# A decoder trunk on one core: projection weights laid out by the host, and one DVE addition per chain replaced by an adding transfer from DRAM

## The chip, the core and the metric

The kernel runs on one core of one Trainium2 chip. The time is device microseconds of one execution, and the kernel is timed several times; the median counts. The engines are called PE (TensorE, the matrix products), PEld (its weight loads, which overlap PE), DVE (VectorE), ACT (ScalarE), POOL (GpSimd) and SP (SyncE). Each works through its own instructions in order. A transfer is issued by SP, ACT or POOL and then done by the 16 DMA engines; "landing" is the moment at which a transfer's completion can be seen.

## The reference

Two layers over 512 tokens of 1024 features, all in float32. Layer 0 mixes tokens by attention, layer 1 by a gated linear recurrence; after each comes a gated feed-forward part with a causal convolution. Cut to what the change touches:

```python
def dilated_attention_mixer(x, w_qkv, w_o, rel_bias):
    qkv = (x @ w_qkv).reshape(B, S, N_GROUPS, 3, HEADS_PER_GROUP, HEAD_DIM)
    ...
def rglru_mixer(x, w_in, ...):
    h = x @ w_in
    ...
def conv_ffn(x, w_up, conv_w, conv_b, w_down):
    u = causal_dwconv(x @ w_up, conv_w, conv_b)      # w_up: 1024 x 6144
    g, v = u[..., :D_FF], u[..., D_FF:]
    return (jax.nn.gelu(g, approximate=True) * v) @ w_down

def reference(...):
    for layer in range(DEPTH):                       # DEPTH = 2
        h = rms_norm(x, norm_mix_pre[layer])
        h = dilated_attention_mixer(h, ...) if layer % 2 == 0 else rglru_mixer(h, ...)
        x = x + rms_norm(h, norm_mix_post[layer])
        h = conv_ffn(rms_norm(x, norm_ffn_pre[layer]), ...)
        x = x + rms_norm(h, norm_ffn_post[layer])
    return x
```

## The kernel before

**Three passes per product.** A weight block of 128 x 512 float32 numbers is split in two: ACT copies it to a rounded high part (`whi`, L169), DVE subtracts that from the block and so gets the low part (`wlo`, L170). Activations are split in the same way. Each product is three matmuls, high by high, high by low and low by high.

**Chunks and their plan.** The weights come in chunks of 1 MB, 8 KB in each of the 128 partitions, in a fixed order (`plan`). `load()` issues a chunk's transfer on SP into a tile `raw`, of which there are three; a chunk may be loaded once the chunk three before it has been split to the end. For a column chunk (`w_cols`) a tile holds 256 columns of the weights: 8 pieces of 256 numbers (1 KB) in a partition. For the attention's columns this takes two transfers per chunk. `pump()` takes the next piece of a chunk and emits its split; there are 14 half buffers for split parts.

**The chains.** In each feed-forward part, 9 of the 12 column groups, with both halves (gate and value), are computed by `seven()` in 18 chains. A chain takes one chunk, seen as four blocks, 128 columns by 512 rows each: `w11` and `w12` (first 128 columns, upper and lower rows), `s1` and `a22` (last 128 columns, upper and lower rows). Seven block products with sums of blocks stand in for eight. The sums on the weights' side are formed in place in `raw`, in the order of `stream()`:

- `ahead`: `s1` becomes s1+a22, by a transfer that reads the block a22 from DRAM and adds it to what lies in SBUF (POOL issues it, L206);
- `left`: once `w11` is split, `w11` becomes w11+s1 by another such transfer;
- the piece `s1` is split, and then `across` makes `s1` the sum of w11 (by now w11+s1) and a22, on DVE (L230);
- the piece `s2` is the split of that sum; after it `lower` adds it to `w12` on DVE (L234), for the piece `s4`.

**What sets the order.** The order is written out: `AT` and `CYCLE` give each of a chain's seven product steps a slot (12 matmuls each), `free_slots` fills the slots between with other work, and at each slot `tick()` emits the next splits. The chains 3 to 8 have nine used slots, the others ten. So DVE's, ACT's and POOL's orders are fixed when the program is built. The step that multiplies `a22` adds to a bank of PSUM after DVE has read that bank at L1100; PE's line is L1082, and ACT copies partial results out at L1091. L812, L816 and L834 are the convolution and the activation that follow a chain, L838 the product of gate and value.

Of the kernel before, what the change touches and what calls it, by code (L numbers as in the profile page):

```python
# [15 lines left out]
ALU = mybir.AluOpType  # L16
AX = mybir.AxisListType

P = 128
S = 512  # L20
D = 1024
KD = D // P
HEADS = 8
HD = 128
D_FF = 3 * D
# [13 lines left out]
SEVEN = range(3, 12)  # L39
# [14 lines left out]
def _bucket(dist):  # L54
    max_exact = BUCKETS // 2
    d = np.maximum(dist, 1).astype(np.float64)
    large = max_exact + (
        np.log(d / max_exact) / np.log(MAX_DISTANCE / max_exact) * (BUCKETS - max_exact)
    ).astype(np.int32)
    large = np.minimum(large, BUCKETS - 1)  # L60
    return np.where(dist < max_exact, dist, large).astype(np.int32)


def _runs(g):

    at, step, n, dist = ((128, 1, 129, 1), (256, 1, 128, 4), (256, 4, 32, 16))[g]
    b = _bucket(np.arange(n) * dist)
    runs, i = [], 0
    while i < n:
        k = i + 1  # L70
        while k < n and b[k] == b[i]:
            k += 1
        if k == i + 1:
            while k < n and b[k] == b[k - 1] + 1 and (k + 1 == n or b[k + 1] != b[k]):
                k += 1
            runs.append((at + i * step, step, k - i, int(b[i]), True))
        else:
            runs.append((at + i * step, step, k - i, int(b[i]), False))
        i = k
    return runs  # L80


@with_exitstack
def kernel(
# [25 lines left out]
    nc = tc.nc  # L110
# [61 lines left out]
    plan = []  # L172
    state = {"dma": 0, "cv": 0, "used": 0, "live": 0, "next": 0, "hold": False, "even": False, "quiet": False}
# [3 lines left out]
    def parts_of(kind, raw):  # L177

        if kind == "feat":
            return [raw[:, :, m * P : (m + 1) * P] for m in range(2)]  # L180
        if kind == "value":
            return [raw[:, 2 * i : 2 * i + 2, :] for i in range(raw.shape[1] // 2)]
        if kind == "rows":
            return [raw[:, i : i + 1, :] for i in range(2)]
        return [raw]
# [11 lines left out]
    def blocks(i):  # L197

        raw = raws[i]
        return {  # L200
            n: raw[:, 4 * k : 4 * k + 4, m * P : m * P + P]
            for n, m, k in (("w11", 0, 0), ("w12", 0, 1), ("s1", 1, 0), ("a22", 1, 1))
        }

    def add_rows(to, src):
        nc.gpsimd.dma_start(to, src, accum_op=ALU.add)  # L206

    def ahead(i):
        assert i < state["dma"]
        add_rows(blocks(i)["s1"], plan[i][3][0][0][:, 4:8, P:256])  # L210

    def free_slots(n):

        end = CYCLE * n
        free = [CYCLE * c + r for c in range(n) for r in ((6, 7, 9) if c < 3 or c > 8 else (6, 7))][2:] + [end, end + 1]
        assert not {CYCLE * c + a for c in range(n) for a in AT.values()} & set(free)
        return free

    def stream(i0, n):

        items = []
        for c in range(n):
            i, o = i0 + c, CYCLE * c

            def left(i=i):
                add_rows(blocks(i)["w11"], plan[i][3][0][0][:, 0:4, P:256])

            def across(i=i):
                x = blocks(i)
                nc.vector.tensor_tensor(x["s1"], x["w11"], x["a22"], op=ALU.add)  # L230

            def lower(i=i):
                x = blocks(i)
                nc.vector.tensor_tensor(x["w12"], x["w12"], x["s1"], op=ALU.add)  # L234

            if c:
                items.append((o - 7, (None, lambda i=i: ahead(i))))
            for at, item in (
                (-6, ("w11", "w11")), (-5.9, (None, left)), (0, ("s1", "s1")), (0.4, ("w12", "w12")),
                (1.5, (None, across)), (5, ("s2", "s1")), (5.1, (None, lower)), (7, ("s3", "w11")),  # L240
                (8.5, ("s4", "w12")), (10.6, ("a22", "a22")),
            ):
                if isinstance(item[0], str):
                    item = ((i, item[0]), lambda i=i, h=item[1]: [blocks(i)[h]], item[0] == "a22")
                items.append((o + at, item))
        free = free_slots(n)
        direct = up["direct"]
        at = 8
        for key, loads, cuts, length in direct:
            u = free[at]  # L250
            if loads:
                items.append((u - EARLY, (None, loads)))
            items.append((u - 1, ((i0, key), cuts, False)))
            at += length
        return [item for _, item in sorted(items, key=lambda x: x[0])]

    def strided_stream(i0):

        items = []
        for r in range(4):  # L260
# [27 lines left out]
            for u in range(4):  # L288
                i = i0 + 6 * r + 4 + u // 2

                def cuts(i=i, m=u % 2):
                    raw = parts_of("value", raws[i])[m]
                    return [raw[:, :1], raw[:, 1:]]

                items.append((ROUND * r + QUARTERS[u if r == 3 else 4 * u], ((i, u % 2), cuts, u % 2 == 1)))
# [124 lines left out]
        while sides:  # L420
            tick()

    def w_cols(w, c0, normed=False, kind="feat"):
        if normed:
            srcs = [(w[i * 512 : (i + 1) * 512, c0 : c0 + 256].rearrange("(p k) c -> p k c", k=4), 4) for i in range(2)]
        else:
            srcs = [(w[:, c0 : c0 + 256].rearrange("(k p) c -> p k c", p=P), KD)]
        plan.append((kind, KD, 256, srcs))

    def w_value(w, *cuts):  # L430

        for i in range(2):
            rows = w[i * 512 : (i + 1) * 512, :]
            plan.append(("value", 4, 512, [(rows[:, c0 : c0 + n].rearrange("(p k) c -> p k c", k=4), n) for c0, n in cuts]))

    def w_rows(w, c):
        r0 = 256 * c
        plan.append(("rows", 2, D, [(w[r0 : r0 + 256, :].rearrange("(k p) c -> p k c", p=P), 2)]) + (True,) * (c == 3))
# [717 lines left out]
    def attention(hT, post, pre):  # L1156
        rowv = [dp.tile([8, TOE], F32, name=f"rowv{g}") for g in range(3)]

        def biases():
            rb = bp.tile([8, 3, BUCKETS], F32, tag="rb", name="rb")  # L1160
            for g in range(3):
                nc.sync.dma_start(rb[:, g], rel_bias[:, 8 * g : 8 * g + 8].rearrange("b h -> h b"))
            yield 1
            for g in range(3):
                row = gen(s="row")[:8, :TOE]
                nc.gpsimd.memset(row, NEG)
                for at, step, n, b, each in _runs(g):
                    src = rb[:, g, b : b + n] if each else rb[:, g, b : b + 1].to_broadcast([8, n])
                    nc.gpsimd.tensor_copy(row[:, at : at + (n - 1) * step + 1 : step], src)
                nc.gpsimd.dma_start(rowv[g], row)  # L1170
                yield 4 if g == 2 else 1
            yield from feature_columns()
# [492 lines left out]
        gate_out(3)  # L1665
        return run()

    qkv, w_in = attn_w_qkv[0], lru_w_in[0]
    for hp in range(4):
        if hp % 2 == 0:  # L1670
            w_value(qkv, (2 * D + hp * 256, 512))
        for j in range(2):
            w_cols(qkv, j * D + hp * 256, True)
    for hp in range(4):
        for g, j in ((1, 0), (1, 1), (2, 0), (2, 1)):
            w_cols(qkv, g * 3 * D + j * D + hp * 256, True, "quad")
        w_value(qkv, *((g * 3 * D + 2 * D + hp * 256, 256) for g in (1, 2)))
    for c in range(4):
        w_rows(attn_w_o[0], c)
    for layer in range(2):  # L1680
        if layer:
            lru_parts = [("x", 0), ("x", 1), ("x", 2), ("g", 0), ("x", 3), ("g", 1), ("g", 2), ("g", 3)]
            for kind, n in lru_parts + [("b", n) for n in range(4)]:
                if kind == "g":
                    plan.append(("gate", 4, 256, [(w[0, n].rearrange("(k p) c -> p k c", p=P), 2) for w in (lru_ga_w, lru_gx_w)]))
                else:
                    w_cols(w_in, n * 256 + (D if kind == "b" else 0))
            for c in range(4):
                w_rows(lru_w_out[0], c)
        for j, half in [(j, half) for j in range(12) for half in range(2)]:  # L1690
            w_cols(ffn_w_up[layer], half * D_FF + j * 256, kind="seven" if j in SEVEN else "feat")
        for half, k in [(1, k) for k in range(0, TAIL, 4)] + [(0, REST[0])] + [(1, k) for k in range(TAIL, 24, 4)]:
            rows = ffn_w_down[layer][k * P : (k + 4) * P, half * 512 : half * 512 + 512]
            plan.append(("value", 4, 512, [(rows.rearrange("(k p) c -> p k c", p=P), 512)]))
# [85 lines left out]
```

## Time and profile before

| | |
|---|---|
| median of 3 runs | 1399.64 us (1399.26 to 1400.11) |
| the profiled execution | 1398.78 us, of which the span is 1397.0 us |
| PE busy | 1383.6 us, 99% of the span |
| PEld, DVE, ACT, POOL busy | 92%, 80%, 57%, 16% |
| granted TensorE clock | 0.999 |
| moved by DMA | 202.05 MB, mean 145 GB/s |

How to read it: the span runs from the first instruction to the last; a busy share is an average over stages, so the stage around the change is read by itself. The attention stage lasts to about 490 us, the first feed-forward part to about 865 us, with its 18 chains on PE from 542 to 782 us; the recurrence to about 1000 us, the second feed-forward part to the end, with chains from 1074 to 1314 us. A row of the timeline gives the start, the time from there to the end, the engine, the line and the instruction, `xN` for N in a row, and in brackets the idle time before it and what ended it. A row of the waits gives the total, the number of times and the longest.

### The profile page before, as it was taken

Reading aid. Unit: us, or ns where it says so; the run is one execution under the profiler, and the core shown is the slowest. Engines: PE = TensorE matmul, PEld = TensorE weight load, DVE = VectorE, ACT = ScalarE, POOL = GpSimd, SP = SyncE. Lnnn points to the kernel's source line nnn. Section 1 sums busy time; section 2 is a strip of 40 time slices with the busy share of each in tenths; the row PEclk is TensorE's granted clock in tenths of the full one; section 3 lists DMA queues with packets and bytes.
Section 4 is the critical chain, followed back from the end, with each engine's and each line's share of the span. In section 5 each row is a group of like instructions: output and inputs, shape, how many; then the busy total and the mean of one; then the engine's idle time right before and its main releaser. Section 6 shows DMA issues by size and latency. Waiting matters only on the chain.

```text
span 1397.0 us, 25641 instructions
## 1 busy us (share of the span) xinstructions
PE 1383.6 (99%) x9797; PEld 1285.1 (92%) x9797; DVE 1121.6 (80%) x2201; ACT 789.7 (57%) x1646; POOL 225.6 (16%) x344
## 2 busy tenths in 40 slices
PE   9999999999999999999999999999999999999998
PEld 7989998999998899999999888989899999999886
DVE  6576898888866889999888759769889999888853
ACT  7343565454536556656666545489556666666641
POOL 0341341222210102212110001000101222111000
PEclk9999999999999999999999999999999999999999
DMA  7644464747574645767663542431444776665511
GB/s 231 180 141 122 122 183 107 222 125 204 147 220 139 204 159 106 165 151 163 133 147 96 185 147 76 136 122 61 151 151 99 161 157 159 160 135 126 175 55 61
DMA packets 171892, 202.05 MB, mean 145 GB/s; under 512 B 10561, under 2 KB 141081, under 8 KB 171513
## 3 DMA queue, kind: packets, MB, share of 16 engines
q1 hardware_dynamic: 123064, 153.34, 34.4%
q0 software_dynamic: 47856, 46.02, 18.1%
q8 instruction: 77, 1.26, 0.4%
q10 hardware_dynamic: 848, 1.05, 0.2%
q14 instruction: 47, 0.38, 0.1%
HBM read 181.41 MB, written 18.96 MB: 143 GB/s over the span
## 4 chain that ended last, share of the span: by engine, by line
PE 82%; DVE 9%; ACT 5%; issue 2%; DMA 1%; POOL 0%; DVEq 0%; ACTq 0%; POOLq 0%
PE ps L1082 29%; PE acc L444 24%; PE ps L444 15%; PE v L1279 7%; DVE wlo L170 4%; ACT whi L169 1%; PE v L1217 1%; DVE u L816 1%; DVE xb L1583 1%; PE O L1491 1%; PE S L1425 1%; PE S L1373 1%; ACT sig L1604 1%; PE tr L537 1%; PE O L444 0%
## 5 line engine op out<-in xcount | busy, mean ns | idle before, releaser
L170 DVE TENSOR_TENSOR wlo<-raw,whi 128x512 fp32r<-128x512 f32 x616 | 406.4, 685 | 109.2 <-ACT whi L169 106.6
L169 ACT ACTIVATE whi<-raw 128x512 fp32r<-128x512 f32 x616 | 365.3, 626 | 156.7 <-PE acc L444 51.2
L444 PE MATMUL ps<-hT,whi 128*128 128x256 f32 x1632 | 281.6, 277 | 1.3 <-ACT whi L169 1.3
L444 PEld LDWEIGHTS ps<-hT,whi 128*128 128x128 f32 x1632 | 247.1, 188 | 2.2 <-ACT whi L169 1.5
L444 PE MATMUL ps<-hT,wlo 128*128 128x256 f32 x816 | 225.4, 276 | 0.4 <-DVE wlo L170 0.4
L1082 PE MATMUL ps<-T,whi 128*128 128x256 f32 x1248 | 221.8, 277 | 0.0
L1082 PE MATMUL ps<-hT,whi 128*128 128x256 f32 x1248 | 220.7, 276 | 0.0
L1082 PEld LDWEIGHTS ps<-T,whi 128*128 128x128 f32 x1248 | 191.5, 188 | 3.0
L1082 PEld LDWEIGHTS ps<-hT,whi 128*128 128x128 f32 x1248 | 190.0, 188 | 2.0
L1082 PE MATMUL ps<-T,wlo 128*128 128x256 f32 x624 | 172.5, 276 | 0.0
L1082 PE MATMUL ps<-hT,wlo 128*128 128x256 f32 x624 | 172.1, 276 | 0.0
L206 POOL DMA_DIRECT2D raw<-in_ffn_w_up_dram x72 | 92.8, 1319 | 409.0 <-DVE wlo L170 278.3
L444 PEld LDWEIGHTS ps<-hT,wlo 128*128 128x128 f32 x816 | 153.4, 188 | 0.6 <-DVE wlo L170 0.6
L444 PE MATMUL acc<-whi,ahi 128*128 128x512 f32 x336 | 131.4, 391 | 0.0
L444 PE MATMUL acc<-whi,alo 128*128 128x512 f32 x336 | 131.0, 390 | 0.2
L444 PE MATMUL acc<-wlo,ahi 128*128 128x512 f32 x336 | 130.8, 389 | 0.0
L1082 PEld LDWEIGHTS ps<-T,wlo 128*128 128x128 f32 x624 | 117.2, 188 | 0.0
L1082 PEld LDWEIGHTS ps<-hT,wlo 128*128 128x128 f32 x624 | 117.2, 188 | 0.0
L1279 PE MATMUL v<-whi,hT 128*128 128x512 f32 x320 | 107.0, 397 | 0.0
L1091 ACT ACTIVATE part<-ps 128x256 f32<-128x256 f32 x156 | 59.0, 378 | 79.8 <-PE ps L1082 76.9
L816 DVE SCALAR_TENSOR_TENSOR u<-ps,cols,u 128x511 f32<-128x511 f32 x120 | 89.4, 746 | 4.5 <-ACT u L812 2.4
L812 ACT ACTIVATE u<-ps,cols 128x512 f32<-128x512 f32 x60 | 46.3, 776 | 61.9 <-DVE ps L1095 50.9
(224 smaller groups left out, 2511.4 us busy)
## 6 DMA issues: line engine op xcount, KB each, us to landing
raw<-in_ffn_w_up_dram SPq DMA_DIRECT2D x48, 1024.0 KB
raw<-in_attn_w_qkv_dram SPq DMA_DIRECT2D x67, 512.0 KB
raw<-in_ffn_w_up_dram POOLq DMA_DIRECT2D x72, 256.0 KB, 4.9
raw<-in_ffn_w_down_dram SPq DMA_DIRECT2D x14, 1024.0 KB
dw<-in_ffn_w_down_dram SPq DMA_DIRECT2D x40, 256.0 KB
raw<-in_lru_w_in_dram SPq DMA_DIRECT2D x8, 1024.0 KB
turned<-T POOLq DMA_DIRECT2D x26, 256.0 KB, 2.6
ft<-turned POOLq DMA_DIRECT2D x104, 64.0 KB, 5.1
```

What stands on the lines that cost most here:

```text
L169: nc.scalar.activation(hi, raw, AF.Copy)
L170: nc.vector.tensor_tensor(lo, raw, hi.bitcast(F32), op=ALU.subtract)
L206: nc.gpsimd.dma_start(to, src, accum_op=ALU.add)
L444: mm(dst, l[a], r[b], start=start and n == 0, stop=stop and n == 2)
L537: nc.tensor.transpose(ps[:, k * P : (k + 1) * P], xs[i][:, k * P : (k + 1) * P], ident)
L812: nc.scalar.activation(u, ps, AF.Identity, scale=own[:, j : j + 1], bias=cc[:, 48 + j : 49 + j])
L816: nc.vector.scalar_tensor_tensor(u[:, d:], ps[:, : S - d], wc, u[:, d:], op0=ALU.mult, op1=ALU.add)
L1082: mm(dst, W[wa][0][:, k, :], right[n](ha, k), start=n in (1, 5) and k == q == 0, stop=k == 3 and q == 2, skip_group_check=True,)
L1091: later(1, lambda: nc.scalar.activation(to, dst, AF.Copy))
L1217: mm(banks[t], hT[a][:, k, t * P : (t + 1) * P], W[b][k % 2][:, 0, :], start=u == n == 0, stop=u == 3 and n == 5,)
L1279: mm(bank, hT[a][:, k, t * P : (t + 1) * P], W[b][k % 2][:, 0, :], start=(k, a, b) == (0, 0, 0), stop=(k, a, b) == (KD - 1, 1, 0),)
L1373: mm(Sp[a // 2][:, o + lo : o + 256], q[hh][:, a * P : (a + 1) * P], k[hh][:, k0 : (a + 1) * P], start=True, stop=True)
```

## The change

The host now brings three weight arrays into the order in which they are loaded, before the kernel is launched: no arithmetic, only an order. A column chunk is 8 KB in a row for each partition, in 16 pieces of 128 numbers, so that the four blocks of a chain are 2 KB in a row each. The attention's value chunks are laid out too. `load()` then needs one transfer for each chunk, of 8 KB pieces. The first two chunks of the attention are still loaded in parts of one or two rows (`w_part`), now out of 8 KB rows.

In the chains, `across` becomes a third adding transfer: block 0 (w11) is read from DRAM and added to `s1`, which by then holds s1+a22, so the sum is the same three blocks. It needs neither `left`'s result nor DVE. `ahead` and `left` now read 128 pieces of 2 KB, where they read 512 of 512 bytes.

```diff
     def parts_of(kind, raw):
         if kind == "feat":
-            return [raw[:, :, m * P : (m + 1) * P] for m in range(2)]
+            return [raw[:, 8 * m : 8 * m + 8, :] for m in range(2)]
...
         raw = raws[i]
         return {
-            n: raw[:, 4 * k : 4 * k + 4, m * P : m * P + P]
-            for n, m, k in (("w11", 0, 0), ("w12", 0, 1), ("s1", 1, 0), ("a22", 1, 1))
+            n: raw[:, 4 * b : 4 * b + 4, :] for b, n in enumerate(("w11", "w12", "s1", "a22"))
         }
-    def add_rows(to, src):
-        nc.gpsimd.dma_start(to, src, accum_op=ALU.add)
+    def add_block(i, to, b):
+        assert i < state["dma"]
+        nc.gpsimd.dma_start(blocks(i)[to], plan[i][3][0][0][:, 4 * b : 4 * b + 4, :], accum_op=ALU.add)
     def ahead(i):
-        assert i < state["dma"]
-        add_rows(blocks(i)["s1"], plan[i][3][0][0][:, 4:8, P:256])
+        add_block(i, "s1", 3)
...
             def left(i=i):
-                add_rows(blocks(i)["w11"], plan[i][3][0][0][:, 0:4, P:256])
+                add_block(i, "w11", 2)
             def across(i=i):
-                x = blocks(i)
-                nc.vector.tensor_tensor(x["s1"], x["w11"], x["a22"], op=ALU.add)
+                add_block(i, "s1", 0)
...
+    def w_cols(w, kind="feat"):
+        plan.append((kind, 16, P, [(w.rearrange("p (k c) -> p k c", c=P), 16)]))
+    def w_value(w, kind="value"):
+        plan.append(("value", 4, 512, [(w.rearrange("p (k c) -> p k c", c=512), 512)]))
...
+def _column_blocks(w, near):
+    n = w.shape[1] // 256
+    if near:
+        w = w.reshape(2, P, 4, n, 2, P).transpose(3, 1, 4, 0, 2, 5)
+    else:
+        w = w.reshape(2, 4, P, n, 2, P).transpose(3, 2, 4, 0, 1, 5)
+    return w.reshape(n, P, 2048)
...
+    if name == "ffn_w_up":
+        return np.stack([_column_blocks(w, False) for w in a])
```

PE's and ACT's orders stay as they were. DVE loses 36 rows, POOL gains 36. The first place is POOL's order in the chains; a row is one chain's adding transfers (the number in `raw1497` is the chunk's tile, what follows `_` a running number). Before:

```order
L206 DMA raw1471_8282<-in_ffn_w_up_dram 128x4x128 x2
L206 DMA raw1497_8441<-in_ffn_w_up_dram 128x4x128 x2
L206 DMA raw1528_8629<-in_ffn_w_up_dram 128x4x128 x2
```

and with the change:

```order
L248 DMA raw1471_8250<-in_ffn_w_up_dram 128x512 x3
L248 DMA raw1497_8409<-in_ffn_w_up_dram 128x512 x3
L248 DMA raw1528_8597<-in_ffn_w_up_dram 128x512 x3
```

A chain's third transfer, `across`, stands on POOL between this chain's `left` and the next chain's `ahead`.

The second place is DVE's order in the chain with tile `raw1497`, from the split of `s1` (first row) to that of `s2`. Before:

```order
L170 TENSOR_TENSOR wlo1544_8736<-raw1497_8441,whi1543_8735 128x512
L170 TENSOR_TENSOR wlo1549_8756<-raw1497_8441,whi1548_8755 128x512
L170 TENSOR_TENSOR wlo1552_8774<-raw1471_8282,whi1551_8773 128x512
L230 TENSOR_TENSOR raw1497_8441<-raw1497_8441 128x4x128
L170 TENSOR_TENSOR wlo1556_8797<-raw1528_8629,whi1555_8796 128x512
L170 TENSOR_TENSOR wlo1558_8814<-raw1497_8441,whi1557_8813 128x512
```

and with the change:

```order
L212 TENSOR_TENSOR wlo1544_8704<-raw1497_8409,whi1543_8703 128x512
L212 TENSOR_TENSOR wlo1549_8724<-raw1497_8409,whi1548_8723 128x512
L212 TENSOR_TENSOR wlo1552_8742<-raw1471_8250,whi1551_8741 128x512
L212 TENSOR_TENSOR wlo1556_8765<-raw1528_8597,whi1555_8764 128x512
L212 TENSOR_TENSOR wlo1558_8782<-raw1497_8409,whi1557_8781 128x512
```

Only L230 is gone: three splits are left between that of `s1` (`wlo1544`) and that of `s2` (`wlo1558`), the last `a22` of the chain before and the `w11` of the chain after among them.

The third place is SP, one chunk of the attention and one of the chains. Before:

```order
L368 DMA raw263_1475<-in_attn_w_qkv_dram 128x4x256 x2
L368 DMA raw1497_8441<-in_ffn_w_up_dram 128x8x256
```

and with the change:

```order
L408 DMA raw263_1467<-in_attn_w_qkv_dram 128x2048
L408 DMA raw1497_8409<-in_ffn_w_up_dram 128x2048
```

The chunks stand where they stood; the attention's two issues have become one.

More of the change, by code (lines that the diff above doesn't have):

```diff
@@ L80, in _runs, with _qkv_order, _laid_out @@
     return runs
+def _qkv_order():
+    order = []
+    for hp in range(4):
+        if hp % 2 == 0:
+            order += [("value", i, [(2 * D + hp * 256, 512)]) for i in range(2)]
+        order += [("feat", j * D + hp * 256) for j in range(2)]
+    for hp in range(4):
+        order += [("quad", g * 3 * D + j * D + hp * 256) for g in (1, 2) for j in range(2)]
+        order += [("value", i, [(g * 3 * D + 2 * D + hp * 256, 256) for g in (1, 2)]) for i in range(2)]
+    return order
+def _column_blocks(w, near):
[5 more added lines that the diff above has]
+    return w.reshape(n, P, 2048)
+def _laid_out(name, value):
+    a = np.asarray(value)
+    if name == "attn_w_qkv":
+        cols, out = _column_blocks(a[0], True), []
+        for kind, at, *cuts in _qkv_order():
+            if kind == "value":
+                rows = a[0][at * 512 : at * 512 + 512].reshape(P, 4, -1)
+                out.append(np.concatenate([rows[:, :, c0 : c0 + m] for c0, m in cuts[0]], 2).reshape(P, 2048))
+            else:
+                out.append(cols[at // 256])
+        return np.stack(out)
+    if name == "lru_w_in":
+        return _column_blocks(a[0], False)
+    if name == "ffn_w_up":
+        return np.stack([_column_blocks(w, False) for w in a])
+    return a
 @with_exitstack
@@ L421, in drain @@
             tick()
[L423 to L434, printed above, removed]
+    def w_cols(w, kind="feat"):
+        plan.append((kind, 16, P, [(w.rearrange("p (k c) -> p k c", c=P), 16)]))
+    def w_value(w, kind="value"):
+        plan.append(("value", 4, 512, [(w.rearrange("p (k c) -> p k c", c=512), 512)]))
     def w_rows(w, c):
@@ L1666, in lru @@
         return run()
[L1668 to L1677, printed above, removed]
+    for n, (kind, *_) in enumerate(_qkv_order()):
+        (w_value if kind == "value" else w_cols)(attn_w_qkv[n], kind)
     for c in range(4):
@@ L1686 @@
                 else:
-                    w_cols(w_in, n * 256 + (D if kind == "b" else 0))
+                    w_cols(lru_w_in[n + 4 * (kind == "b")])
             for c in range(4):
@@ L1690 @@
         for j, half in [(j, half) for j in range(12) for half in range(2)]:
-            w_cols(ffn_w_up[layer], half * D_FF + j * 256, kind="seven" if j in SEVEN else "feat")
+            w_cols(ffn_w_up[layer, 12 * half + j], kind="seven" if j in SEVEN else "feat")
         for half, k in [(1, k) for k in range(0, TAIL, 4)] + [(0, REST[0])] + [(1, k) for k in range(TAIL, 24, 4)]:
@@ L1771 @@
     for name, value in [(n, inputs[n]) for n in _INS]:
-        a = _np.ascontiguousarray(value)
+        a = _np.ascontiguousarray(_laid_out(name, value))
         arrays[f"in_{name}_dram"] = a
```

## The prediction

> **What bounds the kernel now.** I read the page's first part, then the stretches of 35 us over the whole span, to see where PE is not busy.
>
> ```profile
> span 1397.0 us, 25641 instructions
> PE 1383.6 (99%) x9797; PEld 1285.1 (92%) x9797; DVE 1121.6 (80%) x2201; ACT 789.7 (57%) x1646; POOL 225.6 (16%) x344
> ```
>
> PE is idle for 1397.0 - 1383.6 = 13.4 us of the span. Nothing in the change touches PE's own work, so 13.4 us is the most it could ever bring. The stretches show where they are (columns: stretch, its length, busy us and instructions of PE, PEld, DVE, ACT, POOL, then granted clock, DMA share, GB/s):
>
> ```profile
> 0.00:35.00 35.00, 33.15 (x148) 25.74 (x149) 22.95 (x59) 26.25 (x72) 1.63 (x7) 1.00 0.77 230
> 175.00:210.00 35.00, 34.40 (x275) 33.27 (x274) 32.20 (x65) 20.97 (x49) 14.41 (x26) 1.00 0.62 183
> 210.00:245.00 35.00, 33.98 (x223) 30.55 (x223) 28.56 (x88) 19.12 (x58) 6.49 (x12) 1.00 0.42 110
> 595.00:630.00 35.00, 34.52 (x263) 32.65 (x263) 33.38 (x55) 21.87 (x42) 6.85 (x6) 1.00 0.66 151
> 665.00:700.00 35.00, 35.00 (x266) 33.22 (x265) 29.60 (x48) 21.45 (x41) 5.17 (x4) 1.00 0.59 123
> 1120.00:1155.00 35.00, 34.51 (x270) 32.86 (x269) 32.77 (x54) 21.29 (x41) 6.42 (x5) 1.00 0.64 135
> 1365.00:1400.00 35.00, 25.16 (x112) 20.49 (x110) 13.21 (x37) 6.00 (x18) 0.00 (x0) 0.91 0.16 61
> ```
>
> The start (1.85 us) and the end (32.0 - 25.16 = 6.84 us up to 1397.0) are outside the change. Inside the chains PE loses only 0.48 and 0.49 us, at 595 to 630 and 1120 to 1155, and in the attention 0.60 and 1.02. The waits say for what:
>
> ```profile
> PE ps L1082 <- DVE ps L1100: 2.5, 4, 1.0
> ACT whi L169 <- DVE raw L230: 14.9, 14, 2.5
> ```
>
> (Total, times, longest.) The first row is the step on `a22`, which may write its bank of PSUM only after DVE's L1100 has read it. DVE is thus not the bound of the kernel, but in the chains it runs only a little ahead of PE. The second row is the one the change takes hold of: the split of `s2` waits on ACT for DVE's L230.
>
> **The change part by part.** *What DVE loses.*
>
> ```profile
> L230 DVE TENSOR_TENSOR raw<-raw 128x512 f32<-128x512 f32 x36 | 24.6, 684 | 0.0
> ```
>
> 36 additions of 0.684 us, 24.6 us in all, 12.3 in each feed-forward part. The operation lies between the split of `s1` and that of `s2`. What takes its place there is a chain of its own: the split of `s1` ends on DVE, POOL sees it and issues `across`, the transfer lands, ACT splits `s2`, DVE follows. Each link has a row:
>
> ```profile
> 686.64 1.29 DVE L170 TENSOR_TENSOR wlo<-raw,whi 128x512 fp32r<-128x512 f32 x2 [0.92 <-ACT whi L169]
> 687.69 1.30 POOL L206 DMA_DIRECT2D raw<-in_ffn_w_up_dram  x1 [6.74 <-DVE wlo L170]
> 701.70 0.63 ACT L169 ACTIVATE whi<-raw 128x512 fp32r<-128x512 f32 x1
> 702.36 0.69 DVE L170 TENSOR_TENSOR wlo<-raw,whi 128x512 fp32r<-128x512 f32 x1
> ```
>
> The first of the two DVE splits is a `w11`; it ends at 686.64 + 0.69 = 687.33, and POOL's `left`, which waits for it, begins at 687.69: 0.36 us. From ACT's start to DVE's start it is 702.36 - 701.70 = 0.66 us, and I add 0.02 for ACT's start behind a landing.
>
> *How long `across` takes.* No transfer of this shape stands in the trace. The nearest are these: the old adding transfer with the queues free (at 513 us: 1.33 us of issue, 4.4 us to landing), the issue of a plain transfer with as few pieces (`turned`, 128), and what a DMA engine needs for a packet (share x 16 engines x length / packets):
>
> ```profile
> L206 POOL DMA_DIRECT2D raw<-in_ffn_w_up_dram x1: 1326/1326/1326, 513.7 to 513.7; - x1
> DMA to landing us min/median/max: 4.4/4.4/4.4
> L490 POOL DMA_DIRECT2D turned<-T x34 | 18.7, 551 | 356.4 <-DVE T L484 354.7 <-issue 1.4
> q0 software_dynamic: 808, 0.40, 81.6%
> q1 hardware_dynamic: 928, 0.95, 90.2%
> q1 hardware_dynamic: 826, 1.86, 36.6%
> ```
>
> The three queue rows are from 707 to 711, 686 to 689.2 and 786 to 800 us. The first gives 0.816 x 16 x 4 / 808 = 64.6 ns for an added piece of 512 bytes; the second 0.902 x 16 x 3.2 / 928 = 49.8 ns for a plain packet of 1 KB; the third 0.366 x 16 x 14 / 826 = 99 ns for packets of 2252 bytes on average, so 99 x 2048 / 2252 = 90 ns for 2 KB. Old: 512 pieces are 32 for each engine, 32 x 64.6 = 2.07 us, and 4.4 - 1.33 - 2.07 leaves 1.0 us for the rest. New: 128 pieces are 8 for each engine. An added piece reads twice; 512 bytes plain would be at most the 49.8 ns of 1 KB, so the add costs at least 64.6 - 49.8 = 14.8 ns. I take two reads and this: 2 x 90 + 14.8 = 195 ns, 8 x 195 = 1.56 us. With 0.55 us of issue (L490's) the landing is 0.55 + 1.56 + 1.0 = 3.11 us. From both sides: an added piece as cheap as a plain one, 8 x 90 = 0.72, gives 2.27; time in proportion to bytes, 4 x 64.6 = 258 ns, 2.07 us, gives 3.62; nothing gained by longer pieces, 4.4. I take the middle one since the second read must cost something and the per-piece part must shrink with fewer pieces.
>
> The Trainium skill ("Collectives: The Full Stack", section "The bandwidth ceiling: the fold count and why AG ≠ RS ≠ AR") says that an adding transfer is slow not for the addition, but because it needs two source reads. By that alone a piece would be 2 x 90 = 180 ns, the landing 2.99 us and the time about 1413; no row here separates read from add.
>
> *From the end of `s1`'s split to the start of `s2`'s on DVE*, the new distance is 0.36 + 3.11 + 0.02 + 0.66 = 4.15 us. (Bounds, from the three landings above: 3.31, 4.66, 5.44.) The old one stands on DVE's timeline. First and last of 14 chains, and between them one pair of chains:
>
> ```profile
> 582.23 0.68 DVE L170 TENSOR_TENSOR wlo<-raw,whi 128x512 fp32r<-128x512 f32 x1
> 585.45 0.69 DVE L170 TENSOR_TENSOR wlo<-raw,whi 128x512 fp32r<-128x512 f32 x1
> 683.20 0.68 DVE L170 TENSOR_TENSOR wlo<-raw,whi 128x512 fp32r<-128x512 f32 x1
> 688.39 0.69 DVE L170 TENSOR_TENSOR wlo<-dw,whi 128x512 fp32r<-128x512 f32 x1 [0.46 <-ACT whi L169]
> 693.71 0.69 DVE L170 TENSOR_TENSOR wlo<-dw,whi 128x512 fp32r<-128x512 f32 x1 [0.78 <-ACT whi L169]
> 697.89 0.68 DVE L170 TENSOR_TENSOR wlo<-raw,whi 128x512 fp32r<-128x512 f32 x1
> 700.37 0.69 DVE L170 TENSOR_TENSOR wlo<-raw,whi 128x512 fp32r<-128x512 f32 x1 [1.19 <-ACT whi L169]
> 710.67 0.68 DVE L170 TENSOR_TENSOR wlo<-raw,whi 128x512 fp32r<-128x512 f32 x1
> 752.83 0.68 DVE L170 TENSOR_TENSOR wlo<-raw,whi 128x512 fp32r<-128x512 f32 x1
> 757.30 0.69 DVE L170 TENSOR_TENSOR wlo<-raw,whi 128x512 fp32r<-128x512 f32 x1 [0.70 <-ACT whi L169]
> ```
>
> Splits of `s1` begin at 582.23, 683.20, 697.89, 710.67 and 752.83; those of `s2` at 585.45, 687.24 (the second in the row at 686.64), 702.36 and 757.30. The distances are 2.54 (582.91 to 585.45), 3.36, 3.79 and, in the last chain, 3.79; over the 14 chains from 2.5 to 4.0, mean 3.48. The four chains before 582 us I leave out, since DVE has idle time of its own in them to catch up in:
>
> ```profile
> 557.03 1.29 DVE L170 TENSOR_TENSOR wlo<-raw,whi 128x512 fp32r<-128x512 f32 x2 [1.43 <-ACT whi L169]
> ```
>
> If they counted in full, it would be 2 x 4 x 0.67 = 5.4 us more, 1421.
>
> *Does DVE's freed time repay it?* In the pair, the stretches from a start of `s2` to the next end of `s1` are 687.24 to 698.57 = 11.33 us and 702.36 to 711.35 = 8.99 us, together 20.3 of the pair's 27.47. In them DVE is idle for little more than the bracketed 0.46 and 0.78 us, and there ACT is late because it waits for DVE in turn. L230 does not lie in these stretches, so its removal shortens none of them. The idle times that PE causes, 0.92 us (in the row at 686.64) and 1.19 us (at 700.37), lie between `s1` and `s2`: there the new distance swallows them. So each chain's loop of DVE and ACT becomes longer by 4.15 - 3.48 = 0.67 us, and as PE runs with no pause (the stretch 665 to 700 above), the lag adds up: 14 x 0.67 = 9.4 us. Before PE feels it, the margin at `a22` must be used up:
>
> ```profile
> 778.88 0.42 DVE L1100 TENSOR_TENSOR ps<-ps,part 128x256 f32<-128x256 f32 x1
> 780.23 0.39 PE L1082 MATMUL ps<-last,whi 128*128 128x256 f32 x2
> ```
>
> At the last chain it is 780.23 - 779.30 = 0.93 us, and I allow 0.2 for the early chains, whose distance was short for lack of earlier stalls. 9.4 - 0.9 - 0.2 = 8.3 us per feed-forward part. What is late next is L1100, and behind it PE's `a22` step and all of PE. The second part has the same order and the same stall (0.49 beside 0.48), so the sum is 16.6 us.
>
> *The rest at nothing.* `ahead` and `left` issue and land sooner. `across` adds 36 x 0.55 = 20 us to a POOL busy 16%; the next chain's `ahead` behind it on POOL lands some 5 us before ACT reaches its `s1`, about 11 us after this chain's. The attention's loads have one issue instead of two on SP and the same bytes; PE's idle time there (0.60 and 1.02) is put down to L1100, not to a load. If that cover were gone, a later load would show as ACT waiting for a DMA. Splits read contiguous blocks instead of strided ones; both kinds take 0.68 to 0.69 us above (`raw` and `dw`), so nothing.
>
> The sum against the profiled execution: 1398.78 + 16.6 = 1415.4; the median lies 0.86 above that execution, so **1416 us**.
>
> **The rivals.** *Hidden.* If an added piece costs hardly more than a plain one, the distance is 3.31, below today's 3.48: the lag does not grow, and at best the chains' stalls of 0.48 + 0.49 = 0.97 us go: 1398.78 - 0.97 = 1397.8 by this execution, 1398.7 by the median. For it: L230 leaves and the issue shrinks. Against: two reads.
>
> *Faster.* DVE's 24.6 us also clear the stalls of the attention through better loads (0.60 + 1.02) and a part of the recurrence: 1399.6 - 1.0 - 1.6 = 1397.0, and 1396.5 with another 0.5 from there. Against: the attention has no L230.
>
> *A load in the way.* The landing may fall on a running load.
>
> ```profile
> L368 SPq DMA_DIRECT2D raw<-in_ffn_w_up_dram x2: 378/378/378, 685.1 to 701.1; - x2
> q1 hardware_dynamic: 578, 0.75, 107.5%
> ```
>
> The load is issued at 685.1, 1.2 us after the split of `s1` ends (683.88), about when `across` would be moving. The second row is all that moved from 688.5 to 690.5: `left`, issued at 687.69, moves nothing while the load's packets run. A load's piece is now 8 KB, four times 90 ns by bytes, at most 0.40 us. If half of `across`'s 8 pieces wait for one such piece each, that is 1.6 us in every other chain, 0.8 on average, 28 x 0.8 = 22 us more: 1438. Against: `across` is likely half done by then.
>
> The Trainium skill ("DMA: Bandwidth & Descriptors", section "Queues, rings and completion order") says that an engine alternates between its queues packet by packet. By it the pieces interleave with 8 KB ones, as in this rival; the row above, with one queue alone, does not show it.
>
> *The layout doesn't shorten the adding transfer.* At 4.4 us the distance is 5.44, +1.96 per chain: 14 x 1.96 - 1.1 = 26.3 per part, 52.6 in all, 1452. Against: fewer pieces to issue.
>
> **How the numbers follow.** Forecast 0.52 (its own range 1405 to 1432: by the row of bytes 14 x 1.18 - 1.1 = 15.4 per part, 1430; by half the excess of 0.67, 14 x 0.335 - 1.1 = 3.6 per part, 1407), hidden 0.24, load in the way 0.10, no shorter transfer 0.06, faster 0.08. This kernel's measurement can tell about 0.2% (2.8 us) from no change. Slower: 0.52 + 0.10 + 0.06 = 0.68; within 0.2%: 0.24; faster: 0.08. The range goes from the hidden case, 1398, to a little over the load's, 1442.
>
> **What would show it.** Right: the distance from `s1`'s end to `s2`'s start near 4.15 us; `across` landing near 3.1 us; ACT's split waiting for a DMA in most chains; waits of PE's L1082 for L1100's successor that total about 17 us, all from late chains of both parts. Wrong: a distance under 3.5 and no such waits (hidden); landings over 4 us that begin with SP's loads (load in the way); a PE that slows with no wait of its own, which nothing above allows.

## The result, and the profile after

The changed kernel takes 1462.8 us (median, 1460.85 to 1465.2) beside 1399.88 for the kernel before: 62.9 us slower, ratio 1.0445, 95% interval [1.0425, 1.0464]. The forecast was 1416 with a range up to 1442, so the direction was right and the size far off.

The first lines of the page:

```profile
span 1460.4 us, 25661 instructions
PE 1401.4 (96%) x9797; PEld 1292.7 (89%) x9797; DVE 1100.4 (75%) x2165; ACT 781.8 (54%) x1646; POOL 226.2 (15%) x380
```

DVE is busy for 21.2 us less (1121.6 before), as the change meant; PE now idles for 59.0 us instead of 13.4 (its busy time is 17.8 us longer too, at a mean granted clock of 0.994 instead of 0.999). The stretches of 35 us that showed a PE with no pause before show pauses now (same columns as in the prediction; in the second the granted clock is down to 0.95 too):

```profile
665.00:700.00 35.00, 32.99 (x247) 30.74 (x247) 26.61 (x43) 18.45 (x35) 5.21 (x6) 1.00 0.60 151
735.00:770.00 35.00, 28.89 (x199) 26.50 (x198) 21.81 (x36) 16.00 (x32) 5.09 (x7) 0.95 0.52 128
```

The waits name the place:

```profile
ACT whi L211 <- DMA raw<-in_ffn_w_up_dram: 134.9, 36, 7.9
PE ps L1115 <- DVE ps L1133: 31.8, 26, 3.6
PE ps L1115 <- ACT part L1124: 16.4, 17, 4.8
```

ACT waits for one of the transfers 36 times, 134.9 / 36 = 3.7 us each time; 34 of these waits are for `across`, the other two last 0.73 and 0.45 us. Before, the row on L230 had 14.9 us in 14 waits. PE waits for L1133 (L1100 before) 26 times where it waited 4 times, and also, 17 times, for ACT's copies of partial results (L1124), which stand behind the waiting split on ACT. The timeline of one chain (`raw1497`, the same as in the prediction) on DVE, POOL, ACT and DVE:

```profile
701.21 1.28 DVE L212 TENSOR_TENSOR wlo<-raw,whi 128x512 fp32r<-128x512 f32 x2
702.18 0.86 POOL L248 DMA_DIRECT2D raw<-in_ffn_w_up_dram  x1 [11.85 <-DVE wlo L212]
706.87 0.63 ACT L211 ACTIVATE whi<-raw 128x512 fp32r<-128x512 f32 x1 [3.69 <-DMA raw<-in_ffn_w_up_dram]
707.53 0.69 DVE L212 TENSOR_TENSOR wlo<-raw,whi 128x512 fp32r<-128x512 f32 x1 [3.63 <-ACT whi L211]
```

The split of `s1` is the first of the two in the first row and ends at 701.89. POOL issues `across` 0.29 us later, ACT starts on `s2` 4.69 us after that, DVE 0.66 us after ACT: a distance of 5.64 us, where the prediction had 4.15 and the kernel before 3.36. The row of this one transfer, and the landings of all 108:

```profile
L248 POOL DMA_DIRECT2D raw<-in_ffn_w_up_dram x1: 860/860/860, 702.2 to 702.2; - x1
DMA to landing us min/median/max: 4.7/4.7/4.7
...
DMA to landing us min/median/max: 4.1/8.2/10.2
```

The issue takes 0.86 us and the landing 4.7; the prediction had 0.55 and 3.11. The median of 8.2 is that of all three kinds; `left` and `ahead`, which now follow `across` in the same queue, land late, but by the 36 waits above hardly anything waits for them.

**A test of the sum.** I took from the traces, chain by chain, the distance from the end of `s1`'s split to the start of `s2`'s on DVE, and the stretch from there to the next end of `s1`'s split. For the last 14 chains of a part the stretch that leads to each is 9.51 us before and 9.55 and 9.53 after: not touched, as predicted. The distance is 3.48 before, 5.92 (first part) and 5.53 (second part) after. Put into the prediction's sum, 14 x (distance - 3.48) - 1.1 for each part: 33.1 + 27.6 = 60.7 us. Measured: 62.9. So the sum held once the measured distance is in it. Distance and stretch together are all of a chain's time on DVE, so what is tested here is that the stretch stays and that PE has no slack. On POOL and ACT the distance is mostly 0.30 us to the issue, then the landing, 0.02 to ACT's start and 0.66 to DVE's; only the landing differs much from the prediction. The experiments ask what makes up the landing, and whether anything else in the change costs time.

### The profile page after: what moved, and what is told of

The parts are those of the page before. It is cut to its first block, busy times and chain, and to the rows that moved or that the text cites. A ratio compares the mean times of both kernels' runs of the same rounds, so it can differ in the third digit from the quotient of the medians.

```text
span 1460.4 us, 25661 instructions
## 1 busy us (share of the span) xinstructions
PE 1401.4 (96%) x9797; PEld 1292.7 (89%) x9797; DVE 1100.4 (75%) x2165; ACT 781.8 (54%) x1646; POOL 226.2 (15%) x380
## 4 chain that ended last, share of the span: by engine, by line
PE 47%; DMA 22%; issue 18%; DVE 6%; ACT 5%; POOL 2%; POOLq 0%; DVEq 0%; ACTq 0%
DMA raw<-in_ffn_w_up_dram 20%; PE acc L477 17%; PE ps L1115 9%; PE ps L477 8%; PE v L1312 7%; DVE wlo L212 2%; POOL raw L248 2%; PE v L1250 1%; DVE xb L1616 1%; ACT whi L211 1%; PE O L1524 1%; PE S L1458 1%; ACT sig L1637 1%; DMA ft<-turned 1%; PE S L1406 1%
## 5 line engine op out<-in xcount | busy, mean ns | idle before, releaser
L211 ACT ACTIVATE whi<-raw 128x512 fp32r<-128x512 f32 x616 | 365.1, 626 | 268.5 <-DMA raw<-in_ffn_w_up_dram 134.9
L1115 PE MATMUL ps<-T,whi 128*128 128x256 f32 x1248 | 227.3, 281 | 16.5 <-ACT part L1124 16.4
L1115 PE MATMUL ps<-last,whi 128*128 128x256 f32 x416 | 79.4, 289 | 31.8 <-DVE ps L1133 31.8
L1115 PEld LDWEIGHTS ps<-last,whi 128*128 128x128 f32 x416 | 64.4, 191 | 38.0 <-DVE ps L1133 37.6
```

The lines of the kernel that those rows point to most:

```text
L211: nc.scalar.activation(hi, raw, AF.Copy)
L1115: mm(dst, W[wa][0][:, k, :], right[n](ha, k), start=n in (1, 5) and k == q == 0, stop=k == 3 and q == 2, skip_group_check=True,)
```

## The experiments

Theory A: all of the loss is the landing of `across`, on the path between two splits. Theory B: the 8 KB pieces of the loads, or the traffic of the queues, slow the chains by themselves. The kernel before, timed beside the experiments, gave 1400.96 us (e1 to e4) and 1401.54 us (e5 to e8).

### e1: the layout alone

```diff
 def across(i=i):
-    add_block(i, "s1", 0)
+    x = blocks(i)
+    nc.vector.tensor_tensor(x["s1"], x["w11"], x["a22"], op=ALU.add)
```

> The changed kernel with `across` back on DVE (L230's addition), everything else laid out and loaded as changed. Theory A (all of the loss is the landing of `across` between the splits of s1 and s2): no loss, 1397 to 1402 us, distance from the end of s1's split to the start of s2's near 3.5 us. Theory B (the 8 KB pieces of the loads hold up the adding transfers `ahead` and `left`, which land 8 to 10 us after their issue in the changed kernel, and ACT or DVE waits for those): over 1410 us, with waits of DVE or ACT for a transfer.

Measured: 1402.1 us, ratio 1.0009 [1.0001, 1.0018]. Two stretches of its span:

```profile
210.00:245.00 35.00, 32.92 (x196) 29.07 (x195) 26.99 (x86) 17.75 (x55) 6.49 (x12) 0.95 0.30 100
665.00:700.00 35.00, 35.00 (x257) 32.85 (x256) 29.96 (x49) 22.77 (x43) 5.16 (x6) 1.00 0.62 170
```

In the chains PE has no pause (second row), and the distances are those of before to the hundredth, 3.48. The 1.1 us that remain are under the 0.2% that can be told from no change; the first row, from the attention, has 1.1 us less of PE than the same stretch before (33.98), at a lower clock. This profiled execution is the slowest of the twelve (1404.45), and nearly all that it loses lies before the chains, which begin 5.5 us later; the changed kernel, with the same attention, has 33.29 us in that stretch. By itself the layout is neither a gain nor the loss.

### e2: the adding transfer alone

The kernel before, with its old layout, and only this:

```diff
 def across(i=i):
-    x = blocks(i)
-    nc.vector.tensor_tensor(x["s1"], x["w11"], x["a22"], op=ALU.add)
+    add_rows(blocks(i)["s1"], plan[i][3][0][0][:, 0:4, 0:P])
```

> The kernel before, in its old layout, with `across` as an adding transfer of 512 pieces of 512 bytes. Theory A: the landing is 4.4 us at best and 4.9 in the middle as the trace of before has it for such transfers, distance 0.3 + 4.9 + 0.7 = 5.9, so 2 x (14 x (5.9 - 3.48) - 1.1) = 66 us more than before, about 1465. Theory B: the old layout has no 8 KB pieces, so at most the bare landing of 4.4 remains, distance 5.4, 1452 or less.

Measured: 1515.99 us, ratio 1.0822 [1.0805, 1.084]. Far over both expectations. The distances are 7.21 and 7.46 us; the sum gives 51.1 + 54.6 = 105.7 of the 115.0 us measured. Here a second thing shows. One `across` and what the queues moved from 699.3 to 700.5 us, and then from 700.5 to 705:

```profile
L206 POOL DMA_DIRECT2D raw<-in_ffn_w_up_dram x1: 1293/1293/1293, 697.3 to 697.3; - x1
DMA to landing us min/median/max: 7.8/7.8/7.8
...
q1 hardware_dynamic: 163, 0.17, 82.9%
...
q1 hardware_dynamic: 836, 0.86, 65.6%
q0 software_dynamic: 626, 0.31, 54.9%
```

q0 is POOL's queue, q1 SP's. For over a microsecond after the adding transfer should have begun to move, only SP's transfers did; then both shared the engines. The Trainium skill ("DMA: Bandwidth & Descriptors", section "Queues, rings and completion order") has an engine alternate between its queues packet by packet, where a packet holds several descriptors, typically 9 to 17. The last two rows agree with it. The one before need not contradict it: 163 pieces are some 10 for each of 16 engines, but no run here shows where a packet in that sense ends. From the records of single pieces in the trace I set the landing of each adding transfer before which POOL had been idle for over 2.5 us (42, most of them `across`) beside what SP's queue moved from the end of the issue until 0.3 us before the landing:

```
SP moved meanwhile   transfers   mean landing, us
0 to 32 KB              12            4.62
32 to 128 KB             4            4.47
128 to 300 KB            7            4.95
300 to 600 KB            8            5.92
over 600 KB             11            7.91
```

A straight line through them is about 4.5 us + 0.92 x the time that SP's packets took (per DMA engine), with a correlation of 0.99. In the changed kernel the line is 4.23 + 0.94 x SP's time (correlation 0.91), but only 4 of 39 such transfers meet over 300 KB, here 19 of 42. A landing that is late for any reason also leaves more time for SP's packets, so the line alone doesn't tell cause from effect.

The order of the first pieces tells more. In the changed kernel an adding transfer's first piece mostly moves 1.57 us after POOL's start, here 2.0; issuing 128 pieces takes 0.86 us and 512 take 1.28. SP issues the next chunk's load about 0.9 us after `across` in most late chains of both kernels (698.14 here, 703.14 there). Here 11 of the 42 transfers move their first piece only after 2.7 to 4.2 us, with SP's pieces moving before it, and land after 7.9 us in the mean; the other 31 land after 5.0. In the changed kernel this happens once. So the layout's half a microsecond is worth 28 x 0.43 = 12 of the 53 us between 1516 and 1463 by itself; the rest fits `across` moving first there.

### e3: the same transfer, with time to land

```diff
-(1.5, (None, across)), (5, ("s2", "s1")), (5.1, (None, lower)), (7, ("s3", "w11")),
+(1.5, (None, across)), (5, ("s3", "w11")), (7, ("s2", "s1")), (7.1, (None, lower)),
```

> The changed kernel, with the split of s3 emitted ahead of that of s2 (and of `lower`), so that `across` has about 9 us on DVE's order where it had 4.5. Theory A: `across` is hidden, PE has hardly a wait in the chains, 1397 to 1400 us. If something else than the place of `across` slows the chains (queue traffic on POOL, the loads, the buffers of split parts): over 1410 us.

Measured: 1406.51 us, ratio 1.0043 [1.0031, 1.0055]. The first part's stretches:

```profile
525.00:560.00 35.00, 33.98 (x299) 33.79 (x298) 31.34 (x49) 18.26 (x33) 6.04 (x7) 1.00 0.48 119
560.00:595.00 35.00, 34.64 (x295) 33.97 (x294) 30.02 (x48) 22.64 (x43) 7.86 (x9) 1.00 0.65 156
595.00:630.00 35.00, 33.65 (x270) 32.44 (x269) 31.39 (x51) 23.67 (x45) 7.83 (x9) 1.00 0.69 164
665.00:700.00 35.00, 35.00 (x257) 32.90 (x257) 29.35 (x47) 23.38 (x43) 6.08 (x7) 1.00 0.77 189
735.00:770.00 35.00, 35.00 (x254) 32.73 (x253) 29.71 (x47) 21.40 (x40) 4.48 (x6) 1.00 0.64 158
```

Neither number was hit: of the 62.9 us, 57 are gone (5.5 are left), and PE has no pause in the later chains, though the transfer, its landing and its queue traffic are all still there. In the early chains PE loses 1.02 + 0.36 + 1.35 us, again in waits for L1133 and for ACT's copies; that the new order is too late for it there would fit, and e8, which leaves the early chains as they were before, loses none of it. The loss was the place of the transfer.

### e4: a copy in place of the addition

```diff
 def across(i=i):
-    add_block(i, "s1", 0)
+    nc.gpsimd.dma_start(blocks(i)["s1"], plan[i][3][0][0][:, 0:4, :])
```

> The changed kernel with `across` as a plain copy of the block w11 onto s1 (the addition to s1+a22 is left out). If the add costs a second read, a piece of 2 KB takes 84 ns as in the loads instead of 178, 8 x 0.094 = 0.75 us less to landing, distance 4.8 instead of 5.55: 2 x (14 x (4.8 - 3.48) - 1.1) = 35 us over before, 1434 to 1442 with the few late landings. If issue and the queue's own delay set the landing, less than 0.3 us shorter and over 1450.

Measured: 1444.17 us, ratio 1.03 [1.0284, 1.0315]; distances 5.07 and 5.00, the sum gives 41.4 of the 43.2 us. The copies:

```profile
L270 POOL DMA_DIRECT2D raw<-in_ffn_w_up_dram x36: 568/568/571, 539.5 to 1331.5; - x36
DMA to landing us min/median/max: 3.4/3.9/5.7
```

The time lies just above the first expectation's range and well under the second's 1450. The issue of a copy takes 0.57 us, that of an addition 0.86: the prediction took its 0.55 from a copy. The shortest landing is 3.4, for an addition 4.1, so the addition costs 0.7 us here, 0.3 in the issue and 0.4 in the moving; the 0.75 that was expected had all of it in the moving. The pieces are not the same either: the trace records the copy as 64 packets of 4 KB, the addition as 128 of 2 KB. In the packet records a piece of 2 KB takes 84 ns copied by SP and 178 ns added (medians), 2.1 times as long. The two source reads that the Trainium skill ("Collectives: The Full Stack", section "The bandwidth ceiling: the fold count and why AG ≠ RS ≠ AR") names for the add of a ReduceScatter agree with that. They set the price of a packet, not that of the landing.

### e5 and e6: lighter loads beside it

The old layout with the transfer (e5, after e2) and the changed kernel (e6), with most chain chunks loaded only in part, into the tile of three chunks before:

```diff
+light = kind == "seven" and i > RAW_BUFS and plan[i - RAW_BUFS][0] == "seven"
+if light:
+    raw = raws[i - RAW_BUFS]
+    nc.sync.dma_start(raw[:, 12:14, :], srcs[0][0][:, 12:14, :])   # e5: [:, 7:8, 128:256]
...
```

That leaves an eighth of a chunk in e6 (half of the block a22) and a sixteenth in e5.

> The kernel of e2 (old layout, `across` by transfer), with 15 of the 18 chain chunks of each part loaded in a sixteenth only (a part of a22; the rest of the tile keeps the chunk of three before, so other data). Theory A: in e2 the landings of 5.2 to 9 us come from SP's load, which starts 1.2 us after the end of s1's split and whose packets go ahead of `across`; without it every landing is near 4.5 us, distance 5.55, 2 x (14 x (5.55 - 3.48) - 1.1) = 56 us over before, about 1456 instead of 1516. If the queue of the adding transfers itself (`left` and `ahead` right behind `across`) is what makes them late: still over 1490.

> The changed kernel with the same chunks loaded in an eighth of one block only. Theory A: the few late landings (distances of 6 to 10 us) go, the rest shrinks a little, distance about 5.2 (landing 4.2 with the queues free), 2 x (14 x (5.2 - 3.48) - 1.1) = 46 us over before, 1446. If loads play no part: 1460 or more.

Measured: e5 1496.34 us (1.0681 [1.0664, 1.0697]), e6 1462.9 us (1.0443 [1.0426, 1.0459]). Distances 6.91 and 6.80 in e5 (sum 92.3, measured 94.8), 5.70 and 5.63 in e6 (sum 59.0, measured 61.4). For the changed kernel theory A's part on the loads fell: without the chunk loads it is just as slow, as expected if loads play no part (1460 or more). The very late landings did go (none of 45 transfers meets over 300 KB of SP's), but those that meet 32 to 300 KB now take 4.70 us in the mean (24 of them) instead of 4.52 (19), and the mean distance hardly moves, 5.67 instead of 5.73. SP issues the 256 KB loads of `dw` right behind a chunk's load; that these come sooner and take its place would fit, but is not shown.

For the old layout the load is a part, 20 of the 115 us, and 1496 is what was expected of the rival there, the queue of the adding transfers itself (over 1490). Both show in the records of e5. Only 4 of 42 transfers still move their first piece after 3.2 us and land after 8.5 in the mean; all four stand in the last two chains of a part, where SP's load was not cut. The other 38 land after 5.06, much as in e2. And of the transfers that meet 0.7 to 1.1 us of SP's packets, the nine before whose landing POOL's queue moves up to 600 pieces (512 are their own) land after 4.92 us, the six with over 700 after 6.13: there the transfers behind `across` move while it is still under way. That fits the rival, but a late landing also leaves more time for them. How the rest divides between SP's other loads and POOL's queue is open; neither was removed.

### e7: half the transfer

Even chains: 64 partitions instead of 128. Odd chains: all partitions, half of the block's columns.

```diff
-    add_block(i, "s1", 0)
+    to, src = blocks(i)["s1"], plan[i][3][0][0][:, 0:4, :]
+    if c % 2:
+        to, src = to[:, 0:2, :], src[:, 0:2, :]
+    else:
+        to, src = to[0:64], src[0:64]
+    nc.gpsimd.dma_start(to, src, accum_op=ALU.add)
```

> The changed kernel with `across` cut to half a block (the other half of the sum is left out): in even chains 64 pieces of 2 KB, in odd chains 128 pieces of 1 KB. If issue and the time per piece are what the landing is made of: 0.45 us of issue and 4 pieces per engine, landing 2.4 to 2.8 us for the first kind, 0.86 and 8 shorter pieces, 2.8 to 3.3 us for the second; mean distance about 3.8, time 1404 to 1415. If a fixed delay makes up the landing: both over 3.5 us, over 1430.

Measured: 1431.82 us, ratio 1.0224 [1.0207, 1.024]; distances 4.49 and 4.62, the sum gives 27.9 of the 30.3 us. All 36, one of the first kind and one of the second:

```profile
L275 POOL DMA_DIRECT2D raw<-in_ffn_w_up_dram x36: 821/846/878, 536.5 to 1315.1; - x36
DMA to landing us min/median/max: 3.2/3.4/4.1
...
L275 POOL DMA_DIRECT2D raw<-in_ffn_w_up_dram x1: 870/870/870, 572.2 to 572.2; - x1
DMA to landing us min/median/max: 3.2/3.2/3.2
...
L275 POOL DMA_DIRECT2D raw<-in_ffn_w_up_dram x1: 827/827/827, 584.0 to 584.0; - x1
DMA to landing us min/median/max: 3.4/3.4/3.4
```

Half the pieces or half of each piece: the issue stays near 0.85 us and the landing is 3.2 to 3.4 both times, one microsecond less than a whole one. Neither expectation holds: the time is over the second's 1430, but the landings are under its 3.5. As an estimate from the two sizes (4.1 us at the shortest for a whole block, 3.2 for half), some 2.2 us of the landing are fixed, and the rest goes by bytes, not by pieces.

### e8: early chains on DVE, later ones by transfer with time to land

```diff
+LATE = 6
 def across(i=i, c=c):
+    if c < LATE:
+        x = blocks(i)
+        nc.vector.tensor_tensor(x["s1"], x["w11"], x["a22"], op=ALU.add)
+    else:
         add_block(i, "s1", 0)
...
-(1.5, (None, across)), (5, ("s2", "s1")), (5.1, (None, lower)), (7, ("s3", "w11")),
+(1.5, (None, across)), (5 + s, ("s2", "s1")), (5.1 + s, (None, lower)), (7 - s, ("s3", "w11")),   # s = 2 * (c >= LATE)
```

> The changed kernel with DVE's addition in the first six chains of each part and, in the other twelve, `across` by transfer with s3's split ahead of s2's. Theory A: `across` is hidden, the early chains no longer stall, within 0.2% of before: PE had nothing to gain from DVE's 16 us. If DVE's freed time is worth something: over 0.2% faster. If a transfer more per chain costs something even when hidden: over 0.2% slower.

Measured: 1401.11 us beside 1401.54, ratio 0.9997 [0.9987, 1.0007].

```profile
525.00:560.00 35.00, 35.00 (x312) 35.00 (x311) 33.06 (x54) 20.09 (x37) 5.18 (x6) 1.00 0.42 108
595.00:630.00 35.00, 34.51 (x265) 32.69 (x264) 32.35 (x53) 21.24 (x41) 6.08 (x7) 1.00 0.58 144
735.00:770.00 35.00, 35.00 (x262) 33.06 (x261) 29.24 (x48) 21.68 (x41) 3.47 (x4) 1.00 0.50 132
```

With the transfer hidden and the early chains as before, nothing is lost, and nothing is won either: 24 of the 36 additions of 0.68 us taken off DVE bought no time that can be measured. No version here beats the kernel before.

## Why the prediction was wrong

**What bounds the kernel: right.** PE at 99% left nothing to win; e8 takes the work off DVE without a cost and gains nothing.

**The chain through POOL, DMA and ACT: right.** POOL followed in 0.30 us (0.36 predicted), DVE 0.66 after ACT (0.66).

**The lag that adds up: right.** L230's place was not repaid elsewhere (stretch 9.51 before, 9.54 after), and PE fell behind through L1100's successor (31.8 us of waits) and also through ACT's copies (16.4), which the prediction did not name. Once the measured distance is put in, the sum meets five kernels within 3 us, and e2 within 10 (the distances are those of the profiled execution, the times are medians):

| kernel | distance, us (first, second part) | sum | measured |
|---|---|---|---|
| after | 5.92, 5.53 | 60.7 | 62.9 |
| e4 | 5.07, 5.00 | 41.4 | 43.2 |
| e5 | 6.91, 6.80 | 92.3 | 94.8 |
| e6 | 5.70, 5.63 | 59.0 | 61.4 |
| e7 | 4.49, 4.62 | 27.9 | 30.3 |
| e2 | 7.21, 7.46 | 105.7 | 115.0 |

**The landing of `across`: wrong, and nearly all of the error.** This is the step that failed. It was put at 3.11 us, and the distance at 4.15; measured over both parts the mean distance is 5.73, so 28 x 1.58 = 44 us were missing, of the 46 between 16.6 and 62.9. By the prediction's own terms, with the first adding transfer of the changed kernel (at 513 us, queues free) and its packet records:

- *Issue*, 0.55 us from L490, a copy: 0.86 in the chains. An addition's issue is dearer and does not halve with its pieces: 0.82 for 64 pieces in e7, while a copy recorded as 64 packets takes 0.57 in e4. `turned`, too, is recorded as 64 packets of 4 KB, not as the 128 pieces of the prediction. 0.31 us, 28 x 0.31 = 9 us.
- *Moving*, 8 x 195 ns = 1.56 us: the packet was nearly right (178 ns), but the packets took 2.22 us from the first to the last. The prediction took all engines to be busy from first to last. 0.66 us, 18 us.
- *The rest*, 1.0 us: 1.04, right (4.17 less 2.22 and the 0.91 of issue of this first one).
- *In the chains* the middle landing of the 28 is 4.55 (a distance of 5.54) instead of 4.17 with the queues free, another 0.38 us, 11 us; what of it comes from SP and what from the transfers right behind it in the same queue is open.
- *Late landings* raise the mean distance by another 0.19 us above that middle, 5 us.

Only these last ones are the rival "a load in the way". It was given 22 us. In the chain in which the load did move first (at 734 us), it cost more than the 1.6 us reckoned: the landing took 8.3 us. But that was rare, and without the chunk loads the kernel is just as slow (e6). The pieces did not take turns one by one, as the prediction had it for this rival. And landings over 4 us, its sign of a load in the way, came with the queues free too.

**The bounds were the wrong ones.** The row that was nearest, an adding transfer of the same 256 KB, stood at 4.4 us with the queues free. The rival "the layout doesn't shorten the adding transfer", 1452, had 0.06, and the range ended at 1442, below it; it is the case nearest to what came. The layout did shorten the landing with the queues free, but only from 4.44 to 4.17 us, and in the chains it was 4.55, with late ones on top, so the time lies 11 us above this rival's. The bound "in proportion to bytes" (2.07 us of moving) was the one that held (2.22), and it was taken as an end.

**`ahead` and `left` land sooner: wrong, without a price.** The median landing of all the adding transfers went from 4.9 to 8.2 us; three now stand one behind the other, and in e1, with two, it is 4.8. ACT reaches those blocks later still: only two short waits of the 36 are not for `across`.

## What to carry to other kernels

An engine operation of 0.7 us that lies between two dependent steps is not replaced by a transfer at the price of its bytes: the transfer brings its issue, its start and its completion with it, and the chain has to wait for all of them unless other work is moved in between. Take such a landing whole from the nearest transfer of the same kind and size, and don't cut it by parts that no row has shown to shrink. Where a loop has little slack, the excess is multiplied by its rounds: here 2.25 us a chain became 63.

## What the runs showed of the hardware that was not expected

**Few long pieces leave the DMA engines idle.** The first adding transfer of 256 KB, with the queues free, from 514 to 518.5 us: before (512 pieces) and after (128 pieces). The digits are the engines' busy tenths in 40 slices.

```profile
DMA  0000000000000001599999999999999793000000
q0 software_dynamic: 528, 0.26, 46.9%
```

```profile
DMA  0000000000174399976699986577320000500000
q0 software_dynamic: 144, 0.26, 36.5%
```

With 512 short pieces the engines are full almost from the first slice of the transfer to the last; with 128 long ones they are full only in some, and half empty towards the end. The engines work for less time (36.5% against 46.9%), but it takes as long, 2.2 us against 2.1. So the transfer lands 0.27 us sooner (4.17 against 4.44), which is less than its issue is shorter (0.91 against 1.33).

**An adding transfer's issue** on POOL took 1.28 us for 512 pieces, 0.86 for 128, and 0.82 to 0.88 for 64 pieces or for 128 of half the length; a copy of the same block, recorded as 64 packets of 4 KB, took 0.57.

**The queue whose pieces move first gets far ahead.** Two chains of the changed kernel: all that moved from 735 to 738.5 us, where SP's load came 0.34 us behind `across` (issued at 734.4, landed after 8.3 us), and from 703.7 to 705.7 us, where it came 0.96 us behind (issued at 702.2, landed after 4.7); SP's first piece otherwise moves about 1 us after its issue:

```profile
q1 hardware_dynamic: 95, 0.78, 76.0%
```

```profile
q0 software_dynamic: 83, 0.17, 79.2%
```

In each stretch only one of the two queues moved anything. That SP's load puts off `across` was tested by removal: with the loads cut, late first pieces fall from 11 of 42 to 4 (e2 and e5) and from one to none (the changed kernel and e6). The slope of 0.92 to 0.94 us of landing for each microsecond of SP's packets is a correlation, and a weaker one in e6 (0.76, correlation 0.53).
